# Holding the second and third input transfers of a cross-entropy kernel until the scalar engine has loaded its tables

## The chip, the cores and the metric

The kernel runs on one core of one Trainium2 chip. The metric is the device time of one execution in microseconds (us). Before the change it was 85.47 us (median of 3 runs, 85.46 to 85.61).

## The reference

Cross entropy with label smoothing over 256 rows of 32,000 classes, in float32. With smoothing 0.1, the result for each row is the log of its sum of exponentials, minus a small weight times the sum of its logits, minus a large weight times the logit at the label.

```python
log_probs = logits - np.max(logits, axis=-1, keepdims=True)
log_probs = log_probs - np.log(np.sum(np.exp(log_probs), axis=-1, keepdims=True))
smooth_targets = np.full((batch, num_classes), smoothing / num_classes)
...  # the label's entry gets 1 - smoothing more
return (-np.sum(smooth_targets * log_probs, axis=-1)).astype(np.float32)
```

The input is 256 x 32000 x 4 B = 32.77 MB, and each logit is read once. The kernel can't be faster than that stream.

## The kernel before

Each of the 128 partitions holds two rows. The columns come in tiles that get narrower towards the end, so that little work is left when the last one lands. The sync engine issues the input transfers. Six wide ones use a ring of three buffers. The eight narrow ones have buffers of their own. For every piece the scalar engine computes the exponentials and their sum, and VectorE sums the logits.

```python
WIDTHS = (
    (8000, 8000, 8000, 8000),
    (8000, 6272, 4736, 3648, 2688, 2048, 1536, 1216, 1024, 832),
)
...
    ring = ctx.enter_context(tc.tile_pool(name="ring", bufs=3))
...
        nc.scalar.add_instruction(
            mybir.InstLoadActFuncSet(...)      # tables for exp, ln and copy
...
    def load(w: int, col: int, name: str):
        if w >= RING_MIN:
            xt = ring.tile([P, max(WIDTHS[0])], FP32, name="xt", tag="xt")
        else:
            xt = tail.tile([P, w], FP32, name=name, tag=name)
        nc.sync.dma_start(out=xt[:, :w], in_=x[:, col : col + w])
        return xt
```

A hook moves the first input transfer and the label transfer ahead of the start barrier, so these two are issued at the start of the program. The second and third input transfers follow right after that barrier, since their buffers are empty.

The softmax here doesn't subtract the row's maximum and nothing guards it: scores larger than these inputs give would overflow.

## Time and profile before

| what | before |
|---|---|
| time | 85.47 us; 85.36 us in the profiled run |
| span of the profile | 83.57 us |
| busy: scalar engine, VectorE | 59.9 us, 38.9 us |
| input | 32.77 MB |
| table load on the scalar engine | 0.91 to 2.19 us |
| first work on tiles 1, 2, 3 | 12.14, 21.70, 31.35 us |
| output issued; end of span | 81.40 us; 83.57 us |

The span runs from the first issue to the last record of the closing barrier. It is some 1.8 us shorter than the time, in the profiled run 85.36 - 83.57 = 1.79 us. The scalar engine is busy 72% of the span but sits idle 19.4 us for the wide tiles, so the stream is the bound. The change acts in the first 3 us, long before the scalar engine has data to work on.

### The profile page before, as it was taken

How to read it: one execution, taken by the hardware profiler on the slowest of the kernel's cores; microseconds unless marked ns; L12 is line 12 of the kernel's file. 1: busy time of each engine (PE TensorE's matmuls, PEld its weight loads, DVE VectorE, ACT ScalarE, POOL GpSimd, SP SyncE). 2: the span in 40 equal slices, each digit the busy share in tenths (PEclk: the TensorE clock that was granted, in tenths of full speed). 3: DMA queues.
4: the chain of work that ended last, by engine and by line, in shares of the span. 5: the costliest groups of instructions: out<-in, count | busy, mean ns of one | idle time of the engine just before them, and what ended most of it. 6: DMA issues, size and time to landing. Idle time of an engine off the chain costs nothing.

```text
span 83.6 us, 214 instructions
## 1 busy us (share of the span) xinstructions
PE 1.5 (2%) x4; PEld 0.3 (0%) x4; DVE 38.9 (47%) x52; ACT 59.9 (72%) x45; POOL 7.1 (8%) x13
## 2 busy tenths in 40 slices
PE   0000000000000000000001010000000000000030
PEld 0000000000000000000000000000000000000000
DVE  0000019900595009910497119923936654756760
ACT  5000019992699809994499909998999999999950
POOL 2000009981010000000000000000000000000000
DMA  8979998999899989999999999999999999999400
GB/s 245 414 322 490 460 429 352 475 460 429 353 475 429 444 368 475 460 414 398 444 475 429 398 397 456 432 420 399 426 412 433 430 412 424 411 412 406 179 4 0
DMA packets 2227, 32.78 MB, mean 392 GB/s; under 512 B 433, under 2 KB 434, under 8 KB 946
## 3 DMA queue, kind: packets, MB, share of 16 engines
q1 hardware_dynamic: 2018, 32.77, 92.5%
q10 hardware_dynamic: 144, 0.00, 0.1%
q0 software_dynamic: 64, 0.00, 0.1%
q14 instruction: 1, 0.01, 0.0%
HBM read 32.77 MB, written 0.00 MB: 392 GB/s over the span
## 4 chain that ended last, share of the span: by engine, by line
DMA 84%; ACT 9%; DVE 2%; issue 1%; PE 0%; SPq 0%; DVEq 0%; ACTq 0%
DMA xt<-in_logits_dram 59%; DMA xl<-in_logits_dram 26%; ACT ja L181 9%; DVE jd L169 1%; PE lin_t L191 0%; SPq L163 0%; DVE lin_row L193 0%; DVE res L196 0%; DVE done L270 0%; DVEq L196 0%; DVEq L270 0%; ACTq L181 0%
## 5 line engine op out<-in xcount | busy, mean ns | idle before, releaser
L181 ACT ACTIVATE ja<-xt 128x4000 bf16<-128x4000 f32 (+1 forms) x12 | 40.9, 3408 | 19.4 <-DMA xt<-in_logits_dram 19.4
L169 DVE SCALAR_TENSOR_TENSOR jd<-xt 128x2000 f32<-128x2000 f32 (+1 forms) x12 | 26.1, 2176 | 31.4 <-DMA xt<-in_logits_dram 31.2
L181 ACT ACTIVATE ja<-xl 128x2368 bf16<-128x2368 f32 (+7 forms) x9 | 16.5, 1839 | 0.0
L169 DVE SCALAR_TENSOR_TENSOR jd<-xl 128x1184 f32<-128x1184 f32 (+7 forms) x9 | 10.7, 1184 | 7.3 <-DMA xl<-in_logits_dram 7.1
L123 POOL DMA_INDIRECT gat<-in_logits_dram,flat_idx x2 | 3.9, 1938 | 0.5 <-issue 0.3
L115 POOL TENSOR_TENSOR flat_idx<-rowoff,lab 128x2 int32<-128x2 int32 x1 | 2.0, 1999 | 11.1 <-DMA lab<-in_labels_dram 11.1
L181 ACT ACTIVATION_READ_ACCUMULATOR ja<-xt 128x1 f32 x12 | 2.2, 186 | 0.0
L90 ACT ACT_TABLE_LOAD x1 | 1.3, 1283 | 0.9 <-PEq L293 0.9
L181 ACT ACTIVATION_READ_ACCUMULATOR ja<-xl 128x1 f32 x9 | 1.6, 182 | 0.0
L191 PE MATMUL lin_t<-ident,both 128*1 128x128 f32 x1 | 0.4, 373 | 45.7 <-DVE both L218 45.7
L146 POOL TENSOR_SCALAR xsum<-gat 128x1 f32<-128x1 f32 x2 | 0.4, 214 | 7.3 <-DMA gat<-in_logits_dram,flat_idx 7.3
L193 DVE COPY lin_row<-lin_t 1x128 f32<-1x128 f32 x2 | 0.6, 280 | 0.9 <-PE lin_t L191 0.9
L169 DVE DVE_READ_ACCUMULATOR jd<-xt 128x1 f32 x12 | 1.0, 81 | 0.0
L196 DVE SCALAR_TENSOR_TENSOR res<-lin_row,lse_t 1x128 f32<-1x128 f32 x2 | 0.6, 276 | 0.8 <-PE lse_t L195 0.7
L191 PE MATMUL lin_t<-ident,done 128*1 128x128 f32 x1 | 0.4, 373 | 31.5 <-DVE done L270 31.5
L221 DVE TENSOR_REDUCE both<-esum 128x1 f32<-128x8 f32 x1 | 0.2, 161 | 1.6 <-ACT ja L181 1.6
L195 PE MATMUL lse_t<-ident,lse 128*1 128x128 f32 x2 | 0.7, 373 | 2.4 <-ACT lse L187 2.4
L169 DVE DVE_READ_ACCUMULATOR jd<-xl 128x1 f32 x9 | 0.7, 82 | 0.0
L270 DVE TENSOR_TENSOR done<-done,pair 128x2 f32<-128x2 f32 x2 | 0.3, 160 | 0.2
L189 ACT ACTIVATE lse<-elast,done 128x1 f32<-128x1 f32 x1 | 0.3, 261 | 0.2 <-DVE done L270 0.2
L187 ACT ACTIVATE lse<-both 128x1 f32<-128x1 f32 x1 | 0.2, 203 | 0.2 <-DVE both L221 0.2
masks.py:199 POOL TENSOR_SCALAR_AFFINE_SELECT ident<-ident 128x128 f32<-128x128 f32 x1 | 0.3, 282 | 0.0
(12 smaller groups left out, 1.6 us busy)
## 6 DMA issues: line engine op xcount, KB each, us to landing
xt<-in_logits_dram SPq DMA_DIRECT2D x5, 4000.0 KB, 21.4
xt<-in_logits_dram SPq DMA_DIRECT2D x1, 3136.0 KB, 19.2
xl<-in_logits_dram SPq DMA_DIRECT2D x1, 2368.0 KB
xl<-in_logits_dram SPq DMA_DIRECT2D x1, 1824.0 KB, 28.3
xl<-in_logits_dram SPq DMA_DIRECT2D x1, 1344.0 KB, 31.1
xl<-in_logits_dram SPq DMA_DIRECT2D x1, 1024.0 KB, 33.1
xl<-in_logits_dram SPq DMA_DIRECT2D x1, 768.0 KB, 34.4
xl<-in_logits_dram SPq DMA_DIRECT2D x1, 608.0 KB, 35.4
```

The lines of the kernel that those rows point to most:

```text
L90: nc.scalar.add_instruction(mybir.InstLoadActFuncSet(name=nc.get_next_instruction_name(), act_func_set_id=tbl, ins=[], outs=[],))
L115: nc.gpsimd.tensor_tensor(out=flat_idx[:], in0=rowoff[:], in1=lab[:].rearrange("p (r two) -> p r two", two=2)[:, :, 0:1], op=ALU.add,)
L123: nc.gpsimd.indirect_dma_start(out=gat[:, r : r + 1], out_offset=None, in_=logits[:], in_offset=bass.IndirectOffsetOnAxis(ap=flat_idx[:, r ...
L146: nc.gpsimd.tensor_scalar(out=xsum[:, 0:1], in0=gat[:, r : r + 1], scalar1=label_weight, scalar2=None, op0=ALU.mult,)
L169: return nc.vector.scalar_tensor_tensor(out=jd[:, :h], in0=xp[:, :h], scalar=1.0, in1=xp[:, h:w], op0=ALU.mult, op1=ALU.add, accum_out=out,)
L181: nc.scalar.activation(out=ja[:, :w], in_=xp, func=AF.Exp, accum_out=out)
L189: nc.scalar.activation(out=lse[:], in_=se, func=AF.Ln, bias=se_rest)
L191: nc.tensor.transpose(out=lin_t[:], in_=lin, identity=ident[:])
L193: nc.vector.tensor_copy(out=lin_row[:], in_=lin_t[:])
L195: nc.tensor.transpose(out=lse_t[:], in_=lse[:], identity=ident[:])
L196: nc.vector.scalar_tensor_tensor(out=res[:, :, r : r + 1], in0=lin_row[:], scalar=-c_small, in1=lse_t[:], op0=ALU.mult, op1=ALU.add,)
L270: nc.vector.tensor_tensor(out=done[i + 1][:], in0=done[i][:], in1=pairs[i][:], op=ALU.add)
```

## The change

The intent is to keep the second and third transfers out of the way until the scalar engine has its tables. One element of the second buffer is written by that engine after its table load. The second transfer overwrites this buffer and therefore has to wait. The third is issued behind the second on the same queue.

```diff
+    zero = small.tile([P, 1], FP32, name="zero", tag="zero")
+    nc.vector.memset(zero[:], 0.0)
...
+        if col == WIDTHS[0][0]:
+            nc.scalar.activation(out=xt[:, 0:1], in_=zero[:], func=AF.Copy)
         nc.sync.dma_start(out=xt[:, :w], in_=x[:, col : col + w])
```

## The prediction

> **What bounds the kernel now.** I read the chain that ended last first, because it says in one line which resource sets the end:
>
> ```profile
> DMA 84%; ACT 9%; DVE 2%; issue 1%; PE 0%; SPq 0%; DVEq 0%; ACTq 0%
> ```
>
> and its pieces in order of time (start, duration, what) say which transfers:
>
> ```profile
> 1.30 29.96 DMA xt<-in_logits_dram
> ...
> 38.52 19.17 DMA xt<-in_logits_dram
> ...
> 57.71 21.40 DMA xl<-in_logits_dram
> ...
> 79.38 0.61 DVE jd L169 x2
> ```
>
> The reader is to see that transfers of logits are 84% of the span, that the last lands at 57.71 + 21.40 = 79.11 us, and that what follows, from 79.38, is a short tail of small instructions. The kernel is a stream of 32.77 MB with some microseconds at each end.
>
> Next, the scalar engine's timeline (start, duration, engine, line, operation) gives the landings, because the first work on each buffer starts when it lands:
>
> ```profile
> 0.91 1.28 ACT L90 ACT_TABLE_LOAD   x1 [0.91 <-PEq L293]
> 12.14 3.54 ACT L181 ACTIVATE ja<-xt 128x4000 bf16<-128x4000 f32 x1 [9.94 <-DMA xt<-in_logits_dram]
> ...
> 21.70 3.54 ACT L181 ACTIVATE ja<-xt 128x4000 bf16<-128x4000 f32 x1 [2.41 <-DMA xt<-in_logits_dram]
> ...
> 31.35 3.54 ACT L181 ACTIVATE ja<-xt 128x4000 bf16<-128x4000 f32 x1 [2.50 <-DMA xt<-in_logits_dram]
> ```
>
> Starts in the ring are 12.14, 21.70, 31.35, so 9.6 us per 8000-column tile (128 x 8000 x 4 B = 4.096 MB). From the first landing to the last piece's first instruction at 79.38, 32.768 - 4.096 = 28.67 MB come in 67.2 us: 427 GB/s. The first tile takes 12.14 us, which is 2.5 us more than a tile of the steady stream. The table load is over at 0.91 + 1.28 = 2.19 us and the scalar engine then idles 9.94 us for data. So the table load is not on the path.
>
> The start deserves a closer look, for the change touches nothing else. Busy time by stretches of 0.4 us; the last two columns are the DMA share and GB/s, and both count a packet where it starts (which is why they pass 1):
>
> ```profile
> 0.80:1.20 0.40, 0.00 (x0) 0.00 (x0) 0.00 (x0) 0.29 (x1) 0.18 (x3) 1.00 2.53 720
> 1.20:1.60 0.40, 0.00 (x0) 0.00 (x0) 0.00 (x0) 0.40 (x1) 0.17 (x2) 1.00 1.25 400
> 1.60:2.00 0.40, 0.00 (x0) 0.00 (x0) 0.00 (x0) 0.40 (x1) 0.00 (x0) 1.00 0.28 80
> 2.00:2.40 0.40, 0.00 (x0) 0.00 (x0) 0.00 (x0) 0.20 (x1) 0.00 (x0) 1.00 0.20 80
> ...
> 5.20:5.60 0.40, 0.00 (x0) 0.00 (x0) 0.00 (x0) 0.00 (x0) 0.00 (x0) 1.00 1.87 800
> ```
>
> A packet here is one row piece of 32,000 B. In the first line 720 GB/s x 0.4 us = 288 KB, so 9 packets, and 2.53 x 0.4 us x 16 engines = 16.2 us of packet time: 1.80 us each. The second line gives 5 packets of 1.6 us, the third and fourth one packet each, of 1.8 and 1.3 us. That makes 16, the first packet of each engine. In the steady stream (last line) 10 packets take 1.87 x 6.4 = 12.0 us, 1.2 us each. So first packets are slow (27.3 us for 16, mean 1.70 us, 0.5 us over) and spread (the last engine starts after 2.0 us, the first nine before 1.2 us). Every engine carries the same number of rows, so a late engine stays late and sets the landings. In the best case all start by 1.25 us and take 1.2 us, ending at 2.45 us; now the last engine ends near 2.0 + 1.3 = 3.3 us or a little later. About 1 us is the most that a better start can give.
>
> The issues on the sync engine that fall into this stretch:
>
> ```profile
> 0.92 1.26 SPq L163 DMA_DIRECT2D xt<-in_logits_dram  x2
> 1.30 0.89 SPq L163 DMA_DIRECT2D xt<-in_logits_dram  x1
> ```
>
> The second transfer is issued at 0.92, the third from 1.30 to 2.19, and that one takes 0.89 us where the median ring issue takes 0.33. Its end coincides with the end of the table load, and roughly with the last engine's first packet. Something in these 1.3 us holds up descriptors, and three things are active: the table load, the first packets, and these two issues.
>
> **What the Trainium skill says.** "DMA: Bandwidth & Descriptors", section Specifications, gives a fabric ceiling of 435 GB/s; the stream's 427 GB/s agrees, at 98% of it, so mid-stream there is next to nothing to win. The same page, section "Anatomy of one DMA — SWDGE (gpsimd) path", says that DMA engines do not wait on semaphores and that a wait sits on the issuing sequencer. The SyncE queue here shows it: its own waits sum to 28.0 us on VectorE and 7.6 us on the scalar engine. So the new wait will delay the issue of the second and third transfers, not stop data already queued. "ScalarE: Activation LUTs", section "What ACT_TABLE_LOAD costs", has 1283 ns for the load, plus about 1380 ns of drain, and 186 ns + 0.833 ns per element for an ACTIVATE. The load here takes 1283 ns, exactly that, so the transfers do not slow it now and cannot be made to slow it less; the 4000-element ACTIVATE takes 3.52 us against 0.186 + 3.33 = 3.52. Whether the drain follows the load can't be seen before, since the scalar engine is idle afterwards.
>
> **The change part by part.** It removes nothing from the stream: same bytes, buffers and waits for reuse.
> - One VectorE memset of 128x1: GpSimd's in the profile take 0.10 us, and VectorE is idle until 12.14 us. Off the path, 0.
> - One scalar-engine copy of 128x1, estimated at 0.19 us from the skill's fixed cost. It runs after the table load: from about 2.2 us, or from 0.91 + 2.66 = 3.6 us if the drain counts. Done at 2.4 to 3.8 us. That engine waits for data until 12.14 us. Off the path, 0.
> - The second transfer's issue moves from 0.92 to about 2.5 to 3.8 us, the third's to some 0.4 us later. From the start of an issue to its first packet takes about 1 us (issue at 0.00, first packets in 0.80 to 1.20), so the second tile's descriptors are ready at 3.5 to 4.9 us. The first tile is 8 packets per engine: from a first packet ending at 2.6 to 3.4 us, 7 x 1.2 us more keep every engine fed until 11.0 us at least. Slack is over 6 us; no engine runs dry. Cost 0.
> - The fourth and later transfers wait for buffers that the scalar engine frees from about 19.1 us on, as before. 0.
> - The one possible effect: with the two issues out of the 0.9 to 2.2 us stretch, first packets may start closer together or run nearer 1.2 us. Worth between 0 and 1 us.
>
> Costs sum to 0; gain 0 to 1 us, whatever the descriptors' hold-up depended on these issues.
>
> **The rivals.** (a) Nothing moves: first packets are slow for a reason of their own (cold memory or the table load, both unchanged). For it: later issues disturb little. Eight transfers are issued from 38.9 us on, and the stream holds 420 and 435 GB/s in 40 to 48 and 48 to 56 us. Time stays 85.4 to 85.5 us. (b) The queued descriptors of transfers two and three are what spreads the first packets. For it: the 0.89 us issue and the last first packet after 2.0 us fall together. Against: packets starting before 1.2 us are also slow. Half of the 1 us gives 85.0, all of it 84.5. (c) The queue runs dry between tiles one and two, if the held issue came after 9 us; that would show as several us. The slack of over 6 us speaks against it. (d) The label transfer, which lands at 12.2 us, moves. It is needed for a sum only at 45.5 us, so worth 0 either way.
>
> **Range and chances.** I give rival (a) 0.5, a gain of 0.2 to 0.8 us 0.4, more than that 0.05, and a small loss from a changed phase of the engines 0.05. The mean is some 0.25 us off 85.47, so 85.2 us; the range 84.5 to 85.65 holds the nothing case with its spread (85.46 to 85.61) and most of the gain. Two per cent is 1.7 us, above the 1 us bound for the start, so faster by over 2% gets 0.02; slower needs a dry queue or a disturbed profile: 0.02.
>
> **What would show each step.** The copy should end between 2.4 and 3.8 us and the next issues follow within 0.1 us. The start view decides (a) against (b): the same 16 packets at a mean of 1.70 us, or fewer than 27 us and none after 2.0 us. The first work on the first tile (12.14 us now) should move by the same amount as the end, and the 9.6 us between tiles should not move. I am wrong if the second tile comes more than 9.7 us after the first (a dry queue), if the table load itself moves, or if the gain exceeds 1 us, for then something other than first packets was at work.

## The result, and the profile after

The changed kernel took 85.31 us (median of 6 runs, 85.20 to 85.43) against 85.50 us (6 runs) for the kernel before: ratio 0.9977, interval 0.9962 to 0.9991. The interval leaves out 1 by a hair. The difference of the means is 0.20 us.

The chain of waits of the changed kernel shows how the hold works (start, duration, what; in us):

```profile
0.92 1.28 ACT L90
...
2.21 0.21 ACT xt L169
2.42 0.02 issue
2.44 0.33 SPq L170
2.77 0.05 issue
2.82 28.53 DMA xt<-in_logits_dram
```

The reader is to see the table load ending at 2.20, the copy starting 0.01 us later, and the second transfer issued at 2.44 us in place of 0.92. The third follows at 2.82 us in place of 1.30. The hold does what it was meant to do.

The scalar engine's timeline after (start, duration, engine, line, operation, and in brackets the idle time before it and what ended it):

```profile
12.27 3.54 ACT L188 ACTIVATE ja<-xt 128x4000 bf16<-128x4000 f32 x1 [9.85 <-DMA xt<-in_logits_dram]
...
21.87 3.54 ACT L188 ACTIVATE ja<-xt 128x4000 bf16<-128x4000 f32 x1 [2.45 <-DMA xt<-in_logits_dram]
...
31.43 3.54 ACT L188 ACTIVATE ja<-xt 128x4000 bf16<-128x4000 f32 x1 [2.42 <-DMA xt<-in_logits_dram]
```

The first tile is 0.13 us later than before, not earlier, and the distance between tiles is still 9.6 us. The start by stretches of 0.4 us, after (stretch, its length, busy time of PE, PEld, DVE, ACT and POOL, clock, DMA share, GB/s):

```profile
0.80:1.20 0.40, 0.00 (x0) 0.00 (x0) 0.06 (x1) 0.28 (x1) 0.18 (x3) 1.00 3.04 880
1.20:1.60 0.40, 0.00 (x0) 0.00 (x0) 0.00 (x0) 0.40 (x1) 0.17 (x2) 1.00 0.43 160
1.60:2.00 0.40, 0.00 (x0) 0.00 (x0) 0.00 (x0) 0.40 (x1) 0.00 (x0) 1.00 0.77 240
2.00:2.40 0.40, 0.00 (x0) 0.00 (x0) 0.00 (x0) 0.39 (x2) 0.00 (x0) 1.00 0.00 0
```

By the reading that the prediction used, these are 11, 2 and 3 first packets, and (3.04 + 0.43 + 0.77) x 6.4 us = 27.1 us of packet time, against 27.3 before. No packet starts after 2.0 us now, but the last of the 16 ends at 3.44 us, against 3.45 before (the trace's records of single packets). So the start gained nothing.

Then where do 0.20 us come from? In the profiles everything up to the output is no faster: it is issued at 81.52 us, against 81.40 before. Yet the span ends sooner. Here is the output's issue before, from the timeline, and after it the scalar queue's records of the closing code (line, queue, record, count: shortest, median and longest ns, first and last start):

```profile
81.40 0.32 SPq L274 DMA_DIRECT2D out_dram<-res  x1
```

```profile
L307 ACTq DRAIN  x2: 138/206/273, 80.4 to 83.2; - x2
L307 ACTq EVENT_SEMAPHORE  x2: 17/17/17, 82.8 to 83.5; - x2
```

The same two views after:

```profile
81.52 0.32 SPq L281 DMA_DIRECT2D out_dram<-res  x1
```

```profile
L314 ACTq DRAIN  x2: 8/74/139, 80.8 to 83.0; - x2
L314 ACTq EVENT_SEMAPHORE  x2: 17/17/17, 82.9 to 83.5; - x2
```

Before, the scalar engine passes the first closing barrier at 82.8 us, and its last drain, which the second barrier waits for, starts only at 83.2 us. After, it passes at 82.9 us and drains at 83.0 us. In the trace's records the step from the end of the semaphore to that drain is 0.38 us before and 0.07 us after. The pause of 0.3 us has moved: after, it lies ahead of the first drain (80.8 us, before 80.4), where the engine has only to wait for the output anyway. About half of it is won, because GpSimd's own last drain then ends last, 1.79 us after the output's issue in both traces. From the issue of the output to the end of the span it is 2.168 us before and 2.019 us after, 0.149 us less.

The scalar engine's program has 65 records before and 67 after, namely the copy and one semaphore record more. (A record is one entry of the trace for an engine; its semaphores and drains count.) In both, the pause stands ahead of the 64th record. The profile's table of DMA queues shows one instruction packet (8 KB) within the span before, and two after. In the trace that second packet starts at 83.87 us before, after the end of the span, and at 81.46 us after. Before, no instruction packet is in flight during the pause (82.84 to 83.22 us).

So there were two theories. **Hold:** keeping the two transfers back makes the stream a little better. **End:** the hold is worth nothing, and the longer program of the scalar engine moves a pause out of the closing barrier.

### The profile page after: what moved, and what is told of

Same layout as the page of the kernel before. It is cut to its first block, busy times and chain, and to the rows that moved or that the text cites. A ratio compares the mean times of both kernels' runs of the same rounds, so it can differ in the third digit from the quotient of the medians.

```text
span 83.5 us, 217 instructions
## 1 busy us (share of the span) xinstructions
PE 1.5 (2%) x4; PEld 0.3 (0%) x4; DVE 38.9 (47%) x53; ACT 60.1 (72%) x46; POOL 7.1 (9%) x13
## 4 chain that ended last, share of the span: by engine, by line
DMA 57%; ACT 36%; DVE 2%; issue 1%; PE 0%; SPq 0%; DVEq 0%; ACTq 0%
DMA xt<-in_logits_dram 57%; ACT ja L188 34%; ACT L90 2%; DVE jd L176 1%; PE lin_t L198 0%; DVE done L277 0%; SPq L170 0%; DVE lin_row L200 0%; DVE res L203 0%; ACT xt L169 0%; ACTq L188 0%; DVEq L203 0%; DVEq L277 0%
## 5 line engine op out<-in xcount | busy, mean ns | idle before, releaser
L90 ACT ACT_TABLE_LOAD x1 | 1.3, 1283 | 0.9 <-PEq L300 0.9
```

What stands on the lines that cost most here:

```text
L90: nc.scalar.add_instruction(mybir.InstLoadActFuncSet(name=nc.get_next_instruction_name(), act_func_set_id=tbl, ins=[], outs=[],))
```

## The experiments

Twelve runs were made, in three batches of four with 5 rounds each; within a batch all shared the runs of the kernel before. All were correct. "End" is the time from the issue of the output to the end of the span in the run's profile. The kernel before and its repeat have ends of 2.168 and 2.167 us. "Rings" means the DMA engines' queues of pending packets, not the ring of three buffers.

| run | records | end, us | median, us | ratio to before | interval |
|---|---|---|---|---|---|
| the change, first measurement | 67 | 2.019 | 85.31 | 0.9977 | 0.9962 to 0.9991 |
| r1 copy, no hold | 66 | 2.064 | 85.48 | 0.9987 | 0.9964 to 1.0010 |
| r2 the change again | 67 | 2.021 | 85.17 | 0.9970 | 0.9950 to 0.9989 |
| r3 before again | 65 | 2.167 | 85.40 | 0.9996 | 0.9975 to 1.0018 |
| r4 hold to 8 us | 67 | 2.022 | 85.37 | 0.9983 | 0.9963 to 1.0004 |
| r5 two copies, no hold | 67 | 2.023 | 85.39 | 0.9980 | 0.9958 to 1.0002 |
| r6 hold by VectorE | 66 | 2.068 | 85.30 | 0.9987 | 0.9960 to 1.0013 |
| r7 hold to 13 us | 68 | 2.017 | 87.59 | 1.0261 | 1.0229 to 1.0294 |
| r8 late table load | 66 | 2.212 | 85.38 | 0.9977 | 0.9955 to 0.9999 |
| r9 hold to 13 us, third behind second | 68 | 2.027 | 90.41 | 1.0588 | 1.0569 to 1.0608 |
| r10 the change, third time | 67 | 2.024 | 85.38 | 1.0002 | 0.9986 to 1.0019 |
| r11 two copies again | 67 | 2.024 | 85.28 | 0.9999 | 0.9979 to 1.0019 |
| r12 late table load again | 66 | 2.210 | 85.27 | 0.9983 | 0.9965 to 1.0002 |

### r1: the same copy, without the hold

```diff
-            nc.scalar.activation(out=xt[:, 0:1], in_=zero[:], func=AF.Copy)
+            other = small.tile([P, 1], FP32, name="other", tag="other")
+            nc.scalar.activation(out=other[:], in_=zero[:], func=AF.Copy)
```

> The same memset and the same one-element copy on the scalar engine, but written to a tile of its own, so the second and third transfers are issued from 0.92 us as before. If the hold gives the 0.2 us, this kernel is at the time of before (ratio 1.000 +- 0.001, about 85.5 us). If the added instructions (their place in the program, not their wait) give it, the ratio is about 0.998, as for the change.

Ratio 0.9987, halfway between the two. The interval holds both. The profile was sharper than the clock: with no hold at all, the end is 2.064 us, 0.10 us shorter than before. The scalar queue's records of the closing code show that the pause has left the barrier here too:

```profile
L315 ACTq DRAIN  x2: 14/144/273, 80.6 to 83.2; - x2
L315 ACTq EVENT_SEMAPHORE  x2: 17/17/17, 83.1 to 83.7; - x2
```

In the trace's records the last drain starts 0.08 us after its semaphore. With 66 records, the place ahead of the 64th lies in the wait for the output, where a pause can't be seen. So one record more is enough to move it.

### r2 and r3: the change again, and the kernel before against itself

No edit.

> The change itself once more, on this chip and in these rounds. If the 0.2 us is real, the ratio to before is 0.997 to 0.999 again and its interval stays below 1. If it was the luck of six runs, the interval holds 1.000. The 16 first packets should again take about 27 us in sum and the last of them end near 3.44 us.

> The kernel before against itself: measures what a difference of nothing looks like. Both theories expect a ratio within 0.001 of 1; if it comes out 0.002 off with an interval that leaves out 1, then differences of that size between two programs mean nothing here.

The change came out at 0.9970 and the kernel before at 0.9996. The first packets of r2 summed to 29.0 us and the last of them ended at 3.52 us (28.2 and 3.53 us in r3), so the second kernel's start isn't better. With the ends equal to the first profiles' within 0.002 us, the end is a property of the program and not of the run.

### r4: the hold made longer

```diff
-            nc.scalar.activation(out=xt[:, 0:1], in_=zero[:], func=AF.Copy)
+            nc.scalar.activation(out=xt[:, 0:6600], in_=zero[:].to_broadcast([P, 6600]), func=AF.Copy)
```

> The hold made longer: the scalar engine writes 6600 elements into the second buffer in place of one, so the copy should end near 2.2 + 0.19 + 6600 x 0.833 ns = 7.9 us and the second issue follow at 8.0 us. If the first tile keeps all engines fed until 11 us and an issue needs 1 us to its first packet, nothing is lost: the second tile's first work stays at 21.7 to 21.9 us and the time within 0.2 us of the changed kernel, 85.2 to 85.5 us. If the rings need queued work earlier than that, the second tile comes late by the difference, up to 5 us.

The timeline shows the long copy and the two issues after it:

```profile
2.22 5.70 ACT L169 ACTIVATE xt<-zero 128x6600 f32<-128x6600 f32 x1
7.95 0.81 SPq L170 DMA_DIRECT2D xt<-in_logits_dram  x2
```

The second transfer was issued 7.0 us later than before, and the time is 0.9983 of before. In this profile the first tile's work starts at 12.68 us, late already, and the second tile's at 22.27 us. That is outside the expected 21.7 to 21.9 us, but the distance of 9.6 us between them is that of the stream. The rings did not run dry: the trace's records have at least 13 packets in flight at any time from 3.6 to 16 us, where 16 is the usual number. At least 7.95 - 2.44 = 5.5 us of the change's slack is real.

### r5 and r6: the scalar program without the hold, and a hold without the copy

r5 issues the copy of r1 twice. r6 takes out the tile of zeros and the copy, and holds with VectorE:

```diff
-            nc.scalar.activation(out=xt[:, 0:1], in_=zero[:], func=AF.Copy)
+            nc.vector.memset(xt[:, 0:1400], 0.0)
```

> No hold, but two one-element copies on the scalar engine into a tile of its own, so that its program is as long as in the changed kernel (67 records in the trace, against 65 before and 66 with one copy). Theory of the end: the scalar engine's 0.3 us pause in the last barrier moves ahead of its first drain, the time from the issue of the output to the end of the span is 2.02 us (2.168 before), and the time is 0.15 us under before, ratio 0.997 to 0.999. Theory of the hold: nothing is held, so the ratio is 1.000 +- 0.001.

> A hold of the same sort with the scalar engine's program left as it was before: VectorE writes 1400 elements into the second buffer, which should keep the second issue back to about 2.4 us. Theory of the end: 65 records on the scalar engine, 2.168 us from output issue to the end, ratio 1.000 +- 0.001. Theory of the hold: ratio 0.997 to 0.999, as with the change.

r5 went as the theory of the end has it, with 67 records, an end of 2.023 us and ratio 0.9980, although its interval just reaches 1. r6 didn't have the program that was wanted. A semaphore record was added on the scalar engine, which made 66, so its end is 2.068 us and it can't stand for the old end. It is usable in another way. It holds (second issue at 2.54 us) and r1 does not, both have 66 records and ends within 0.004 us, and both are at 0.9987 of before. The hold between them is worth nothing that shows.

### r7: a hold past the first tile

The copy is replaced by two, of 8000 and of 4600 elements.

> The hold made longer than the first tile: 12,600 elements in two copies, so the second issue falls at about 2.2 + 0.19 + 12600 x 0.833 ns + overlap = 13.0 us and its first packets start 1 us later. The engines finish the first tile near 11.0 to 11.8 us, so by the theory of slack the rings are empty for some 2.2 to 3 us: the second tile's first work moves from 21.8 to 24 to 25 us and the time to 87.6 to 88.5 us. If the rings were kept busy by something else, less.

The time of 87.59 us is at the edge of what was expected, but not for the reason expected. The third transfer, which waits for nothing, was issued at 0.92 us, ahead of the held one, and kept the rings busy. The held second tile landed behind it. The scalar engine's next tile after the first shows it:

```profile
31.51 3.54 ACT L189 ACTIVATE ja<-xt 128x4000 bf16<-128x4000 f32 x1 [11.33 <-DMA xt<-in_logits_dram]
```

Work on the second tile starts at 31.51 us in place of 21.70, after 11.33 us of idling, since tiles are consumed in order. Its buffers came free late, and near 39.5 us the rings ran out of work for a moment: the packets in flight fall from 16 to 9. What follows that gap answers another question. Stretches of 0.4 us, columns as above:

```profile
39.20:39.60 0.40, 0.00 (x0) 0.00 (x0) 0.40 (x1) 0.40 (x1) 0.00 (x0) 1.00 0.19 80
39.60:40.00 0.40, 0.00 (x0) 0.00 (x0) 0.40 (x1) 0.40 (x1) 0.00 (x0) 1.00 2.11 560
```

560 GB/s x 0.4 us = 224 KB is 7 packets, and 2.11 x 6.4 = 13.5 us is 1.93 us each. Packets are as slow here as at the start of the program, with the table load 37 us in the past. By the trace's records the first 16 after the gap take 27.2 us in sum, 1.70 us each, as the first 16 of the program do. In these two places slow packets came where rings restarted.

### r8: the table load moved

The cut leaves out that the label transfer is moved ahead of these lines.

```diff
+    for _ in range(3):
+        busy = junk.tile([P, PIECE // 2], FP32, name="jd", tag="jd")
+        nc.vector.memset(busy[:], 0.0)
+    gate = small.tile([P, 1], FP32, name="gate", tag="gate")
+    nc.vector.memset(gate[:], 0.0)
+    opened = small.tile([P, 1], FP32, name="opened", tag="opened")
+    held = nc.scalar.dma_start(out=opened[0:1, :], in_=gate[0:1, :])
-    if tbl is not None:
+    with tc.issue_after(held.ins):
         nc.scalar.add_instruction(...)        # the table load
```

> The table load moved to about 5 us or later, behind a one-element transfer that waits for three memsets on VectorE; the second and third transfers are issued at once, as before. If the table load slows the first packets and the third issue (0.89 us before), the 16 first packets fall from 27 to 29 us in sum to about 20 us, the last of them ends before 3 us, the third issue takes 0.33 us and the first tile's work starts before 11.9 us. If it has nothing to do with it, the sum stays at 27 to 29 us, the third issue at 0.8 us or more and the first tile at 12.1 to 12.4 us.

```profile
1.32 0.82 SPq L170 DMA_DIRECT2D xt<-in_logits_dram  x1
```

```profile
4.42 1.28 ACT L103 ACT_TABLE_LOAD   x1 [4.42 <-issue]
...
12.42 3.54 ACT L188 ACTIVATE ja<-xt 128x4000 bf16<-128x4000 f32 x1 [6.71 <-DMA xt<-in_logits_dram]
```

The table load runs from 4.42 us and the third issue still takes 0.82 us (first fence). The first tile is at 12.42 us, and the first packets sum to 30.0 us (27.0 us in the repeat, r12). So the table load has nothing to do with either. The ratio of 0.9977 was a surprise, since the end is 0.04 us longer than before. The trace shows why it is longer. With 66 records the pause has left the barrier here too (0.08 us from the semaphore to the last drain). But the sync engine's wait for the output is now the third of its six closing waits and no longer the last, and three more follow it at 0.06 us each.

### r9: the long hold with the order kept

```diff
+        if col == 2 * WIDTHS[0][0]:
+            with tc.issue_after(issued[-1].ins):
+                issued.append(nc.sync.dma_start(out=xt[:, :w], in_=x[:, col : col + w]))
+        else:
+            issued.append(nc.sync.dma_start(out=xt[:, :w], in_=x[:, col : col + w]))
-        nc.sync.dma_start(out=xt[:, :w], in_=x[:, col : col + w])
```

> The long hold once more, with the third transfer made to follow the second (in the run before this one the third was issued first, at 0.92 us, and kept the rings busy). The second issue falls at 13.05 us, its first packets at 14.1 us; the engines finish the first tile between 11.0 and 11.8 us. The rings should then show no packet starting in between, and the packets that restart the stream should be slow as at the start (1.5 to 2 us in place of 1.2), since the table load is long over. The second tile's work starts at 24.5 to 25.2 us (21.8 before), the time rises by 2.7 to 3.4 us, to 88.1 to 88.9 us. If a late second issue costs nothing even here, the slack in the prediction was the wrong picture.

A miss as well. The third now stayed behind the second (13.55 us), but the schedule let a later, narrower tile pass both at 0.92 us:

```profile
0.92 0.33 SPq L179 DMA_DIRECT2D xl<-in_logits_dram  x1
...
13.17 0.33 SPq L179 DMA_DIRECT2D xt<-in_logits_dram  x1
```

```profile
28.04 3.54 ACT L197 ACTIVATE ja<-xt 128x4000 bf16<-128x4000 f32 x1 [7.86 <-DMA xt<-in_logits_dram]
```

The rings didn't run dry here either, and the last input packets end at 79.2 us in the trace, 0.5 us after the 78.7 of before. Yet the kernel takes 5 us more. The scalar engine idled 7.86 us for the second tile and worked off the backlog after the stream had ended: its last piece starts at 85.13 us (79.24 before). What a dry ring between tiles one and two costs is left open.

### r10, r11 and r12: the close calls once more, side by side

No edits against the change, r5 and r8.

> The changed kernel beside the one with two copies and no hold, in the same rounds. Theory of the end: both have 67 records on the scalar engine, both end 2.02 us after the output's issue, and their mean times agree within 0.1 us. Theory of the hold: this one is 0.15 us or more under the other. Ratio to before 0.997 to 0.999.

> Two copies and no hold, again. Theory of the end: ratio 0.998, within 0.001 of the changed kernel's in these rounds. Theory of the hold: 1.000.

> The late table load again, because its first run was 0.23% under before although its end is 0.04 us longer (2.212 us), which the theory of the end does not explain. If that theory covers everything, the ratio is now 1.000 to 1.001. If it is 0.998 again, something other than the end moves times by this much, and the cause of the change's 0.2 us is only settled in part.

The change with the hold and the two copies without it agree: means 85.36 and 85.35 us in the same rounds, with ends of 2.024 us both. That is what the theory of the end asks for; the theory of the hold wanted 0.15 us between them. But this time both were level with the kernel before (1.0002 and 0.9999) and neither had its 0.15 us. Their ends were as short as ever, and the spread from run to run (a standard deviation of 0.09 to 0.21 us, r7 and r9 left out) is as large as such a difference. And the late table load was at 0.9983 again, 0.10 us under before by its mean, with an end 0.04 us longer. Its interval reaches 1, so either something other than the end moves times by that much, or this too is spread.

## Why the prediction was right or wrong

**What bounds the kernel: right.** The stream kept its 9.6 us per tile, and its last packets end at 78.77 us (78.68 before).

**Costs of the parts: right.** The memset took 0.06 us and the copy 0.20 us, both off the path. The copy was done at 2.42 us, the early end of "2.4 to 3.8 us", so no drain followed the table load. The second issue followed 0.02 us later. That no engine runs dry was shown up to an issue at 7.95 us (r4). The slack of "over 6 us" beyond that was not tested, because r7 and r9 let other transfers go first.

**Rival (a), nothing moves at the start: right.** (Its time of 85.4 to 85.5 us is missed by 0.1 us.) The first packets summed to 27.1, 29.0 and 27.9 us in the change's three profiles and 27.3 and 28.2 in those of before, and the last ended at 3.25 to 3.52 us against 3.45 and 3.53. Of the two reasons given for it, r8 rules out the table load. r7 shows slow packets at a restart with the tables long loaded; why, no run shows.

**Rival (b), the gain at the start: wrong.** It was given 0.45 and moved the mean by 0.25 us to 85.2. No gain appeared there: the step from "the 0.89 us issue and the last first packet after 2.0 us fall together" to issues that spread the packets didn't hold. Without those issues the start is the same. With the table load elsewhere the third issue still took 0.82 us. Two readings were loose as well. The 0.89 us was set against a median of 0.33 us, but later issues that start 0.05 us behind another take 0.43 to 0.48 us in the same profile. And of the "eight transfers" that are to show that later issues disturb little, six are issued by 41.41 us, the others at 50.25 and 57.71 us.

**The term that was missing: the end.** The prediction treated everything after the output as fixed. In the profiles of the change it is 0.144 to 0.149 us shorter, because the records added on the scalar engine move a 0.3 us pause away from the closing barrier. Over the three measurements the change's mean is 0.20, 0.23 and 0.02 us under that of before (over all runs of a batch; the ratios use the same rounds alone), 0.15 on average, which is that size. But the times don't tell short ends from long ones: over all six measurements with 67 records the mean is 0.12 us under before, and over the two with the late table load, whose end is longer, 0.14 us. So 85.2 us came near 85.31 us by luck: the 0.25 us came from a gain at the start, which did not appear.

**What stays open.** That the end is shorter is shown in every profile of the change, and r10 beside r11 shows no worth of the hold. That the end makes up the timed difference, in whole or in part, isn't shown: in that batch both had the short end and neither was faster than before. The late table load is 0.10 to 0.19 us under before in its two batches without a shorter end. What the pause is stays open too. A wait for an instruction packet doesn't fit the kernel before: its packets run from 80.06 to 80.54 us and from 83.87 us on, and the pause lies between them. No version beat both kernels by more than the spread.

## What to carry to other kernels

Holding back a transfer whose data is queued behind 10 us of other data bought nothing and cost nothing that these runs resolve, up to an issue at 7.95 us. Where another transfer overtook the held one (r7 and r9), it cost 2 and 5 us. A difference of 0.2% between two versions calls for a look at the closing barrier before the changed lines are credited, since an instruction more on one engine moved a pause out of it here. Compare with a version that has the same number of instructions and lacks the effect.

## What the Trainium skill lacked or had wrong

- "ScalarE: Activation LUTs", section "What ACT_TABLE_LOAD costs", counts about 1380 ns of drain with every switch to a different set. Here the load took 1283 ns as stated, and a copy started 0.01 us after its end. No drain followed this first load of the program. The engine had run no activation before the load, so a drain ahead of it is not excluded.
- "DMA: Bandwidth & Descriptors", section Specifications, gives about 0.6 us to the first byte on this path. Whether it counts from the start or the end of the issue is not said. Counted from the end, it fits at the start of the program: the issue ends at 0.40 us, and the first packets start at 1.02 us. At the restart in r7 it was 0.84 us from the end of the issue (39.02 us) to the first packet (39.86 us).
- I found on no page that packets are slow when rings restart: the first 16 took 1.69 to 1.88 us on average at the start and 1.70 us after the gap in r7, against 1.19 us for the same 32,000 bytes in the stream.
- I found on no page that an issue close behind another holds its queue longer, and at the start longer still: 0.33 us alone, 0.42 to 0.48 us when it started 0.05 us behind another, and 0.78 to 1.02 us for the third issue in the runs with issues at 0.92 and 1.30 us.
- I found on no page the pause of 0.3 us in the scalar engine's queue near the end of the program. Where the traces show it, it stands ahead of the engine's 64th record: inside the closing barrier with 65 records (output to end 2.168 us) and ahead of it with 67 (2.02 us).
